# Where the selection work, the first-product halves and the gathers stand in a one-core PEER layer

## The chip, the cores and the metric

The kernel runs on one core of a Trainium2 chip. TensorE (PE) does the matrix products, VectorE (DVE) and ScalarE (ACT) the elementwise work, GpSimd (POOL) issues the gathers, SyncE (SP) issues the other DMAs; each engine takes its instructions in the order in which they stand. The metric is device microseconds of one execution; lower is better. Before the change the median of three runs is 3994.11 us (3992.14 to 4011.59).

## The reference

One layer is computed for 128 context tokens and 512 sample tokens with D = 2048. A mixer (input projection, a convolution branch, a two-way linear recurrence, output projection) is followed by PEER, a retrieval of experts out of 128 x 128:

```python
q = (xb @ w_query).reshape(TOKEN_BLOCK, PEER_HEADS, 2, D_KEY)
s = jnp.einsum('chpd,hpnd->chpn', q, sub_keys)
sv, si = lax.top_k(s, PEER_TOPK)                       # 16 best of 128 keys, both halves
cand = sv[:, :, 0, :, None] + sv[:, :, 1, None, :]     # 16 x 16 sums
top_s, top_pos = lax.top_k(cand, PEER_TOPK)            # 16 experts per head, 8 heads
ids = jnp.take_along_axis(cand_id, top_pos, axis=-1)
g = jax.nn.softmax(top_s, axis=-1)
act = gelu(einsum('chkd,cd->chk', jnp.take(peer_u, ids, axis=0), xb))
return einsum('chk,chkd->cd', g * act, jnp.take(peer_v, ids, axis=0))
```

Everything is in float32. A layer norm with residual closes each part.

## The kernel before

The tokens are in two groups. For group b (256 tokens, two tiles) experts are selected first; its first 192 tokens are **gathered tokens**: for each of their 128 experts per token a row of `peer_u` and a row of `peer_v` are fetched by indirect DMA (128 rows of 8 KB in one gather; 384 gathers, as the last 64 tokens share two halves of one tile). The other 448 sample tokens (64 of b, 384 of a) are done **densely**: all 16384 experts are multiplied, with a matrix of weights that is zero but for the selected ones.

After the mixer, PE goes through these stages:

1. The **first query** (`query(rpb, ...)`, group b, 32 halves of the query weights), with the output projection of group a between its halves, then the norm of group a.
2. The **second query** (`query(rpa, ...)`, group a, 32 halves; a half is 24 matmuls of 384 columns, lines 88 to 90).
3. The **first product**: 256 halves of `peer_uT` (24 matmuls of 448 columns each, `s_half`, lines 929 to 931). The generator `ahead_gen` issues one half for each `s_next()`. Two halves make one tile of 128 experts; ScalarE applies gelu (line 944) and SP writes the tile to DRAM (line 946). The first halves go to the PSUM tile `mm`, later ones to `sps`.
4. Part of these halves go beside the **one-hot matrices** (lines 977 to 1019): DVE and ACT build one-hot rows, PE multiplies them (line 1014), and the dense weights are written to `g_d` in 14 blocks. How many first-product halves stand between is worked out in line 995 from how many were already issued (`s_first`).
5. The **second product**, 256 halves of `peer_v` (lines 88 to 90 with the tile `vps`), which reads the gelu tiles (`ge`) and the weights (`gt`) back.

Every half of every weight is loaded by SP (line 82, 512 KB), split into a high part by ACT (line 76, `whi`) and a low part by DVE (line 77, `wlo`); PE needs both. There are two buffers of `whi` and `wlo` each, a third one for every third half.

**Selection** is DVE work: `tops` finds the 16 best of 128 keys, `choose` the 16 experts of a head, turns positions into numbers by comparing against 0..15 (`oh`), and writes `ids` and `gts`. It is cut into pieces, generators in a list `chores`; `chore(us)` adds a credit and issues pieces until their nominal costs (the numbers after `yield`) have used it up. The constants `C_WO`, `C_NA`, `C_QA`, `C_S` (line 759) are the credit for one half in each stage. When group b is selected, the piece `b_end` sets `b_done`; from there `pace(rate)` lets out gathers: `R_Q` = 0.4 for each half of the query and of the first product, 0.8 beside the one-hot matrices, and what is left, spread evenly, over the second product (`r_v`, line 1076). A gather of `peer_u` is followed by a dot product on DVE (line 853), one of `peer_v` by a sum on DVE (line 864). Three buffers hold gathered rows, so the third gather issued makes the oldest one be used; a gather also waits until PE has passed the half two before it (`after`, `LAG`).

The framework's scheduler orders the issued instructions on each engine; the order quoted below is the built one.

Of the kernel before, what the change touches and what calls it, by code (L numbers as in the profile page):

```python
# [34 lines left out]
def layer_kernel(ctx: ExitStack, tc: tile.TileContext, i: dict, y_p: bass.AP, y_s: bass.AP, st_o: bass.AP):  # L35
# [34 lines left out]
    def split(raw):  # L70
        n = raw.shape[1:]
        nsplit[0] += 1
        p = wx[0] if wx and nsplit[0] % 3 == 0 else w_p
        hi = p.tile([128, *n], F32R, name="whi", tag="whi")
        lo = p.tile([128, *n], F32R, name="wlo", tag="wlo")
        S.copy(hi, raw)  # L76
        V.tensor_tensor(lo, raw, hi.bitcast(F32), op=ALU.subtract)  # L77
        return hi, lo

    def load_w(src):  # L80
        raw = w_p.tile([128, *src.shape[1:]], F32, name="wraw", tag="wraw", bufs=3)
        Q.dma_start(raw, src)
        return raw
# [29 lines left out]
    def tp_bank():  # L113
        return ps_tp.tile([128, 512], F32, name="tp", tag="tp")

    def mm_bank():
        return ps_mm.tile([128, 512], F32, name="mm", tag="mm")
# [453 lines left out]
    def chore(us):  # L571
        credit[0] += us
        while chores and credit[0] > 0:
            try:
                credit[0] -= next(chores[0])
            except StopIteration:
                chores.pop(0)
        if not chores:
            credit[0] = min(credit[0], 0.0)
# [31 lines left out]
    def top16(rp, vals, idx, src, n):  # L611
        V.max(vals[:, 0:8], src)
        V.max_index(idx[:, 0:8], vals[:, 0:8], src)
        s2 = rp.tile([128, 128], F32, name="s2", tag="s2", bufs=1)
        V.match_replace(s2[:, 0:n], vals[:, 0:8], src, -3.0e38)
        V.max(vals[:, 8:16], s2[:, 0:n])
        V.max_index(idx[:, 8:16], vals[:, 8:16], s2[:, 0:n])

    def tops(rp, tv, ti, s, p, nt):
        for n in range(nt):  # L620
            top16(rp, tv[:, n, p, :], ti[:, n, p, :], s[:, n * 128:(n + 1) * 128], 128)
            yield 1.7

    def choose(rp, h, tv, ti, ts):
        nt = len(ts)

        def rt(shape, name, dt=F32, bufs=2):
            return rp.tile([128, *shape], dt, name=name, tag=name, bufs=bufs)

        cand = rt([nt, 112], "cand", bufs=1)  # L630
        for c0, a0, na, nb in ((0, 0, 4, 16), (64, 4, 12, 4)):
            V.tensor_tensor(
                cand[:, :, c0:c0 + na * nb].rearrange("p t (a b) -> p t a b", a=na),
                tv[:, :, 0, a0:a0 + na].unsqueeze(3).to_broadcast([128, nt, na, nb]),
                tv[:, :, 1, 0:nb].unsqueeze(2).to_broadcast([128, nt, na, nb]), op=ALU.add)
        yield 0.6
        tsv, tsp = rt([nt, 16], "tsv"), rt([nt, 16], "tsp", U32)
        for n in range(nt):
            top16(rp, tsv[:, n, :], tsp[:, n, :], cand[:, n, :], 112)
            yield 1.6  # L640
        nmx = rt([nt], "nmx")
        V.tensor_scalar(nmx, tsv[:, :, 0], -1.0, None, op0=ALU.mult)
        e, z = rt([nt, 16], "e"), rt([nt], "z")
        for n in range(nt):
            S.activation(e[:, n, :], tsv[:, n, :], AF.Exp, bias=nmx[:, n:n + 1], accum_out=z[:, n:n + 1])
        pu = rt([4, nt, 16], "pu", U32, bufs=1)
        pf = rt([4, nt, 16], "pf", bufs=1)
        V.tensor_scalar(pu[:, 0], tsp, 4, None, op0=ALU.logical_shift_right)
        V.tensor_scalar(pu[:, 1], tsp, 15, None, op0=ALU.bitwise_and)
        V.tensor_scalar(pu[:, 2], tsp, 2, None, op0=ALU.logical_shift_right)  # L650
        V.tensor_scalar(pu[:, 3], tsp, 3, None, op0=ALU.bitwise_and)
        S.copy(pf, pu)
        tif = rt([nt, 2, 16], "tif", bufs=1)
        S.copy(tif, ti)
        yield 0.9
        msk = rt([nt, 16], "msk")
        V.tensor_scalar(msk, pf[:, 0], 4.0, None, op0=ALU.is_ge)
        V.tensor_scalar(pf[:, 2], pf[:, 2], -12.0, None, op0=ALU.add)
        V.tensor_tensor(pf[:, 2:4], pf[:, 2:4], pf[:, 0:2], op=ALU.subtract)
        V.tensor_tensor(pf[:, 2:4], pf[:, 2:4], msk.unsqueeze(1).to_broadcast([128, 2, nt, 16]), op=ALU.mult)  # L660
        V.tensor_tensor(pf[:, 0:2], pf[:, 0:2], pf[:, 2:4], op=ALU.add)
        V.reciprocal(z, z)
        hk = slice(16 * h, 16 * h + 16)
        V.tensor_tensor(gts[:, ts[0]:ts[-1] + 1, hk], e, z.unsqueeze(2).to_broadcast([128, nt, 16]), op=ALU.mult)
        yield 1.5
        rs = []
        for p in range(2):
            oh = rt([nt, 16, 16], "oh", bufs=1)
            full = [128, nt, 16, 16]
            V.tensor_tensor(oh, pf[:, p].unsqueeze(3).to_broadcast(full),  # L670
                            iota[:, 0:16].unsqueeze(1).unsqueeze(1).to_broadcast(full), op=ALU.is_equal)
            yield 0.3 * nt
            V.tensor_tensor(oh, oh, tif[:, :, p, :].unsqueeze(2).to_broadcast(full), op=ALU.mult)
            yield 0.3 * nt
            r = rt([nt, 16], "r") if ts[0] == 0 else ij[:, 1:4, p, hk]
            V.tensor_reduce(r, oh, axis=AX.X, op=ALU.add)
            yield 0.3 * nt
            rs.append(r)
        if ts[0] == 0:
            for p in range(2):  # L680
                S.copy(ij[:, 0, p, hk], rs[p][:, 1, :])
            V.scalar_tensor_tensor(rs[0], rs[0], 128.0, rs[1], op0=ALU.mult, op1=ALU.add)
            V.tensor_copy(ids[:, :, hk], rs[0])
            yield 0.4

    def query(rp, uh, ul, ts, step, deep):
        nt = len(ts)
        N = nt * 128
        o = OFF if ts[0] else 0
        late = []  # L690
        for h in range(8):
            kT = rp.tile([128, 2, 128], F32, name="kT", tag="kT", bufs=2)
            Q.dma_start(kT, i["keysT"][:, 2 * h:2 * h + 2, :])
            tv = rp.tile([128, nt, 2, 16], F32, name="tv", tag="tv", bufs=deep)
            ti = rp.tile([128, nt, 2, 16], U32, name="ti", tag="ti", bufs=deep)
            for p in range(2):
                m = 2 * h + p
                bank = mm_bank()

                def scores(bank=bank, h=h, p=p, kT=kT, tv=tv, ti=ti):  # L700
                    qT = rp.tile([128, N], F32, name="qT", tag="qT", bufs=2)
                    S.copy(qT, bank[:, 0:N])
                    tp = tp_bank()
                    for n in range(nt):
                        T.matmul(tp[:, n * 128:(n + 1) * 128], qT[:, n * 128:(n + 1) * 128], kT[:, p, :], start=True, stop=True)
                    s = rp.tile([128, N], F32, name="s", tag="s", bufs=2 * deep - 1)
                    S.copy(s, tp[:, 0:N])
                    chores.append(tops(rp, tv, ti, s, p, nt))
                    if p:
                        chores.append(choose(rp, h, tv, ti, ts))  # L710

                for half in range(2):
                    raw = load_w(i["w_query"][m, :, half * 8:half * 8 + 8, :])
                    wh, wl = split(raw)
                    for kk in range(8):
                        k = half * 8 + kk
                        mk = mm3(bank[:, 0:N], wh[:, kk, :], wl[:, kk, :], uh[:, k, o:o + N], ul[:, k, o:o + N], k == 0, k == KT - 1)
                    marks.append(mk)
                    while late:
                        late.pop(0)()  # L720
                    step(2 * m + half)
                late.append(scores)
        while late:
            late.pop(0)()
# [31 lines left out]
                chores.insert(0, norm_a(*u2_a))  # L756
        chore(C_WO if not u2_a else C_NA)

    C_WO, C_NA, C_QA, C_S = 3.6, 2.8, 2.6, 2.8
    query(rpb, u2hi_b, u2lo_b, TB, step_b, 4)  # L760
    while len(chores) and chores[0].__name__ == "norm_a":
        chore(1.0)
# [9 lines left out]
    b_done = [False]  # L772
# [130 lines left out]
    R_Q, R_A = 0.4, 0.8  # L903
# [5 lines left out]
    def pace(n):  # L909
        if not b_done[0]:  # L910
            return
        due[0] += n
        while due[0] >= 1.0:
            due[0] -= 1.0
            left[0] -= 1
            next(gg, None)
# [18 lines left out]
    rate = [R_Q]  # L935
# [17 lines left out]
    def s_next():  # L953
        next(ag, None)
        nahead[0] += 1

    def step_a(n):
        pace(R_Q)
        chore(C_QA)

    query(rpa, u2hi_a, u2lo_a, TA, step_a, 4)
    while chores:
        s_next()
        chore(C_S)
# [239 lines left out]
```

## Time and profile before

| | |
|---|---|
| median of 3 runs | 3994.11 us (3992.14 to 4011.59) |
| profiled execution | 3995.82 us |
| its span | 3994.0 us |
| mean granted TensorE clock | 0.974 |
| PE busy | 3775.8 us, 95% |
| DVE busy | 3104.1 us, 78% |
| ACT busy | 1577.9 us, 40% |
| mean DMA rate | 264 GB/s |

The profile is of one execution; times in its rows are microseconds from the start of the span. PE busy is not PE at its peak: a matmul of 448 columns counts 369 ns, while back to back one starts about every 201.6 ns (249 in 50 us, or 1135 in 230 us). So lost time on PE is taken here as the length of a stretch less its matmuls at their back-to-back spacing, which also takes in stretches at the lower clock.

### The profile page before, as it was taken

How to read it: one execution, taken by the hardware profiler on the slowest of the kernel's cores; microseconds unless marked ns; L12 is line 12 of the kernel's file. 1: busy time of each engine (PE TensorE's matmuls, PEld its weight loads, DVE VectorE, ACT ScalarE, POOL GpSimd, SP SyncE). 2: the span in 40 equal slices, each digit the busy share in tenths (PEclk: the TensorE clock that was granted, in tenths of full speed). 3: DMA queues.
4: the chain of work that ended last, by engine and by line, in shares of the span. 5: the costliest groups of instructions: out<-in, count | busy, mean ns of one | idle time of the engine just before them, and what ended most of it. 6: DMA issues, size and time to landing. Idle time of an engine off the chain costs nothing.

```text
span 3994.0 us, 53950 instructions
## 1 busy us (share of the span) xinstructions
PE 3775.8 (95%) x20405; PEld 3355.1 (84%) x20405; DVE 3104.1 (78%) x4545; ACT 1577.9 (40%) x2697; POOL 742.3 (19%) x522
## 2 busy tenths in 40 slices
PE   7899899799999999999999999989999999999996
PEld 2688778678889999889998898979898988889886
DVE  5599965667899944688887787868888888888877
ACT  2111354533453322567675666632222222222221
POOL 0000111410000100112121222222332223332300
PEclk8899999899999999999999999999999999999998
DMA  9565444586533666788998788899999999999982
GB/s 365 204 203 182 152 142 161 185 256 227 167 127 111 213 214 216 256 319 302 321 316 301 275 289 306 314 345 357 337 352 330 355 339 333 347 332 358 330 239 89
DMA packets 408885, 1054.89 MB, mean 264 GB/s; under 512 B 27904, under 2 KB 253136, under 8 KB 355424
## 3 DMA queue, kind: packets, MB, share of 16 engines
q1 hardware_dynamic: 353328, 648.76, 48.5%
q0 software_dynamic: 55296, 402.68, 27.2%
q8 instruction: 160, 2.62, 0.3%
q14 instruction: 101, 0.83, 0.1%
HBM read 979.37 MB, written 71.38 MB: 263 GB/s over the span
## 4 chain that ended last, share of the span: by engine, by line
PE 53%; DMA 20%; DVE 15%; issue 7%; ACT 2%; POOL 1%; SPq 0%; DVEq 0%; POOLq 0%; ACTq 0%
PE sps L931 5%; PE sps L929 5%; PE sps L930 5%; PE vps L90 5%; PE vps L88 5%; PE vps L89 5%; DVE wlo L77 4%; DMA wa<-in_w_ada 4%; DMA ge<-ge_d 3%; DMA gt<-g_d 2%; DMA rows<-in_peer_v,ids 2%; DMA wraw<-in_peer_uT 2%; PE mm L931 2%; PE mm L930 2%; PE mm L929 2%
## 5 line engine op out<-in xcount | busy, mean ns | idle before, releaser
L76 ACT CAST whi<-wraw 128x1024 fp32r<-128x1024 f32 x704 | 736.8, 1049 | 1718.4 <-DMA wraw<-in_peer_v 380.9
L77 DVE TENSOR_TENSOR wlo<-wraw,whi 128x1024 fp32r<-128x1024 f32 x704 | 862.1, 1228 | 190.7 <-ACT whi L76 188.9
L853 DVE SCALAR_TENSOR_TENSOR rows<-rows,urow 128x2048 f32<-128x2048 f32 x192 | 439.1, 2287 | 187.2 <-DMA rows<-in_peer_u,ids 166.5
L929 PE MATMUL sps<-u2hi_a,whi 128*128 128x448 f32 x1488 | 548.9, 369 | 14.4 <-ACT whi L76 12.5
L864 DVE SCALAR_TENSOR_TENSOR gacc<-rows,coefs,gacc 128x2048 f32<-128x2048 f32 x190 | 445.9, 2347 | 146.7 <-DMA rows<-in_peer_v,ids 118.2
L931 PE MATMUL sps<-u2hi_a,wlo 128*128 128x448 f32 x1488 | 549.4, 369 | 7.9 <-DVE wlo L77 7.8
L930 PE MATMUL sps<-u2lo_a,whi 128*128 128x448 f32 x1488 | 547.6, 368 | 0.0
L88 PE MATMUL vps<-ehd,whi 128*128 128x448 f32 x1088 | 401.2, 370 | 15.6 <-ACT ehd L1055 10.6
L90 PE MATMUL vps<-ehd,wlo 128*128 128x448 f32 x1088 | 401.8, 369 | 6.8 <-DVE wlo L77 6.8
L89 PE MATMUL vps<-ehd,whi 128*128 128x448 f32 x1088 | 401.0, 369 | 0.0
L820 POOL DMA_INDIRECT rows<-in_peer_u,ids x128 | 184.2, 1439 | 1055.4 <-PE gps L1014 248.6
L90 PE MATMUL vps<-ehl,wlo 128*128 128x448 f32 x960 | 354.2, 369 | 20.8 <-DVE wlo L77 20.8
L88 PE MATMUL vps<-ehl,whi 128*128 128x448 f32 x960 | 352.2, 367 | 2.7 <-ACT whi L76 1.6
L89 PE MATMUL vps<-ehl,whi 128*128 128x448 f32 x960 | 351.9, 367 | 0.0
L929 PEld LDWEIGHTS sps<-u2hi_a,whi 128*128 128x128 f32 x1488 | 282.3, 190 | 38.0 <-ACT whi L76 13.7
L931 PEld LDWEIGHTS sps<-u2hi_a,wlo 128*128 128x128 f32 x1488 | 281.8, 189 | 37.4 <-DVE wlo L77 13.7
L930 PEld LDWEIGHTS sps<-u2lo_a,whi 128*128 128x128 f32 x1488 | 282.1, 190 | 22.2
L820 POOL DMA_INDIRECT rows<-in_peer_v,ids x128 | 197.3, 1541 | 533.9 <-PE gps L1014 162.9
L1010 ACT ACTIVATE A<-ab,gsp,nij 128x128 fp32r<-128x128 f32 x672 | 284.2, 487 | 1.6 <-DVE nij L991 1.5
L88 PEld LDWEIGHTS vps<-ehd,whi 128*128 128x128 f32 x1088 | 205.5, 189 | 35.4 <-ACT ehd L1055 11.0
L90 PEld LDWEIGHTS vps<-ehd,wlo 128*128 128x128 f32 x1088 | 205.4, 189 | 28.9 <-DVE wlo L77 10.9
L332 DVE SCALAR_TENSOR_TENSOR ybuf<-z,par,ybuf 128x655 f32<-128x655 f32 x240 | 220.6, 921 | 6.4
(301 smaller groups left out, 7514.8 us busy)
## 6 DMA issues: line engine op xcount, KB each, us to landing
wraw<-in_peer_uT SPq DMA_DIRECT2D x256, 512.0 KB
wraw<-in_peer_v SPq DMA_DIRECT2D x256, 512.0 KB
wa<-in_w_ada SPq DMA_DIRECT2D x192, 512.0 KB
wraw<-in_w_in SPq DMA_DIRECT2D x64, 512.0 KB
wraw<-in_w_out SPq DMA_DIRECT2D x64, 512.0 KB
wraw<-in_w_query SPq DMA_DIRECT2D x64, 512.0 KB
ge_d<-ge SPq DMA_DIRECT2D x128, 224.0 KB
g_d<-gst SPq DMA_DIRECT2D x14, 2048.0 KB
```

The source lines that it names most:

```text
L76: S.copy(hi, raw)
L77: V.tensor_tensor(lo, raw, hi.bitcast(F32), op=ALU.subtract)
L88: T.matmul(out, ah, bh, start=first, stop=False)
L89: T.matmul(out, ah, bl, start=False, stop=False)
L90: return T.matmul(out, al, bh, start=False, stop=last)
L820: d = G.indirect_dma_start(out=r, out_offset=None, in_=src, in_offset=bass.IndirectOffsetOnAxis(ap=idx, axis=0))
L853: V.scalar_tensor_tensor(r, r, 1.0, u, op0=ALU.mult, op1=ALU.mult, accum_out=dots[:, p:p + 1])
L864: V.scalar_tensor_tensor(acc, r, coef[:, p:p + 1], acc, op0=ALU.mult, op1=ALU.add)
L929: T.matmul(sps, wh[:, kk, :], u2hi_a[:, k, :], start=(k == 0), stop=False)
L930: T.matmul(sps, wh[:, kk, :], u2lo_a[:, k, :], start=False, stop=False)
L931: mk = T.matmul(sps, wl[:, kk, :], u2hi_a[:, k, :], start=False, stop=(k == KT - 1))
L1010: S.activation(A[:, x], ab, AF.Relu, scale=nij[:, 1 + x, n:n + 1], bias=gsp[:, x, n:n + 1])
```

## The change

The nominal costs of selection pieces change a little (a piece of `tops` 1.7 to 1.6, and so on), so a credit issues slightly more. The credit in the first query beside the output projection goes from 3.6 to 5.6. In the second query `step_a` has two cases: until group b is selected it issues a first-product half (`s_next`) and a credit of 8.0 for each query half; after that it lets out gathers and a credit of 3.3 (2.6 before). In the loop behind the query the credit is 4.2 (2.8) and the gather rate 0.45 (0.4).

```diff
@@ tops, choose (nominal costs of the pieces)
-            yield 1.7
+            yield 1.6
...
-            yield 1.6
+            yield 1.5
...
-        yield 0.9
+        yield 0.8
...
-        yield 1.5
+        yield 1.3
...
-            yield 0.3 * nt
+            yield 0.13 + 0.27 * nt
...
@@ -756,7 +756,7 @@
-    C_WO, C_NA, C_QA, C_S = 3.6, 2.8, 2.6, 2.8
+    C_WO, C_NA, C_QB, C_QA, C_S = 5.6, 2.8, 8.0, 3.3, 4.2
     query(rpb, u2hi_b, u2lo_b, TB, step_b, 4)
...
@@ -955,10 +955,15 @@
     def step_a(n):
-        pace(R_Q)
-        chore(C_QA)
+        if b_done[0]:
+            pace(R_Q)
+            chore(C_QA)
+        else:
+            s_next()
+            chore(C_QB)
 
     query(rpa, u2hi_a, u2lo_a, TA, step_a, 4)
+    rate[0] = 0.45
     while chores:
         s_next()
         chore(C_S)
```

In the built order of before, PE in the second query goes from one query half to the next, with the scores of the half-head (line 705) between:

```order
L88 MATMUL mm<-u2hi_a,whi 128x384
L89 MATMUL mm<-u2lo_a,whi 128x384
L90 MATMUL mm<-u2hi_a,wlo 128x384
L705 MATMUL tp<-kT,qT 128x128 x3
L88 MATMUL mm<-u2hi_a,whi 128x384
L89 MATMUL mm<-u2lo_a,whi 128x384
L90 MATMUL mm<-u2hi_a,wlo 128x384
```

In the changed kernel, at the same place on PE (lines 929 to 931 are the first product):

```order
L88 MATMUL mm<-u2hi_a,whi 128x384
L89 MATMUL mm<-u2lo_a,whi 128x384
L90 MATMUL mm<-u2hi_a,wlo 128x384
L705 MATMUL tp<-kT,qT 128x128 x3
L929 MATMUL mm<-u2hi_a,whi 128x448
L930 MATMUL mm<-u2lo_a,whi 128x448
L931 MATMUL mm<-u2hi_a,wlo 128x448
```

Ten first-product halves now stand between the first query halves, one each. In all, 36 halves of the first product come ahead of the one-hot matrices, where 70 did, and 220 beside them, where 186 did.

On DVE the first dot product of a gather (line 853) stands, before the change, behind the second query, among the first-product halves:

```order
L642 TENSOR_SCALAR nmx<-tsv 128x3
L612 MAX tv<-s 128x8
L853 SCALAR_TENSOR_TENSOR rows,dotss<-rows,urow 128x2048
L77 TENSOR_TENSOR wlo<-wraw,whi 128x1024
L616 MAX tsv<-s_13325 128x8
```

In the changed kernel the first one on DVE stands inside the second query, among the pieces of `tops`:

```order
L617 MAX_INDEX ti<-tv,s_11407 128x8
L613 MAX_INDEX ti<-tv,s 128x8
L853 SCALAR_TENSOR_TENSOR rows,dotss<-rows,urow 128x2048
L77 TENSOR_TENSOR wlo<-wraw,whi 128x1024
L615 MATCH_REPLACE s_11443<-tv,s 128x128
```

Counted in splits (line 77) from the first of the second query, the first dot product moves from behind the 38th to behind the 24th, and the last selection piece from behind the 53rd to behind the 61st. Gathers used on DVE ahead of the one-hot stage, beside it and in the second product: 26, 149 and 209 before, 20, 176 and 188 now. The selection instructions on DVE ahead of the first split of the second query are 211 in both.

On SP, in the same query, the loads before stand in fours behind each other:

```order
L82 DMA wraw<-in_w_query 128x1024 x3
L693 DMA kT<-in_keysT 128x256
L82 DMA wraw<-in_w_query 128x1024 x4
L693 DMA kT<-in_keysT 128x256
L82 DMA wraw<-in_w_query 128x1024
```

In the changed kernel SP has the loads of both weights in turn, and writes of gelu tiles (line 946) among them:

```order
L82 DMA wraw<-in_peer_uT 128x1024
L82 DMA wraw<-in_w_query 128x1024
L82 DMA wraw<-in_peer_uT 128x1024
L946 DMA ge_d_9949<-ge 128x448
L82 DMA wraw<-in_w_query 128x1024
L82 DMA wraw<-in_peer_uT 128x1024
```

A write waits for its gelu, and the loads behind it wait with it. ACT holds 18 table loads in the selection stretch, where it held 8.

## Rows read from the trace of the kernel before

**Rows 1.** The page: busy time by engine, and GB/s in 40 slices.
```profile
PE 3775.8 (95%) x20405; PEld 3355.1 (84%) x20405; DVE 3104.1 (78%) x4545; ACT 1577.9 (40%) x2697; POOL 742.3 (19%) x522
...
GB/s 365 204 203 182 152 142 161 185 256 227 167 127 111 213 214 216 256 319 302 321 316 301 275 289 306 314 345 357 337 352 330 355 339 333 347 332 358 330 239 89
```

**Rows 2.** Busy time by stretch: us, engines (instructions), granted clock, DMA share, GB/s.
```profile
core 0: us, PE busy (x) PEld busy (x) DVE busy (x) ACT busy (x) POOL busy (x), PEclk, DMA share, GB/s
1132.00:1286.00 154.00, 148.12 (x862) 146.25 (x863) 152.21 (x651) 61.01 (x139) 0.00 (x0) 0.98 0.37 120
1150.00:1200.00 50.00, 50.00 (x300) 50.00 (x299) 50.00 (x233) 18.53 (x44) 0.00 (x0) 1.00 0.38 125
1286.00:1400.00 114.00, 113.16 (x558) 103.61 (x557) 108.98 (x359) 44.79 (x75) 10.04 (x8) 1.00 0.60 201
1400.00:1630.00 230.00, 230.00 (x1135) 212.78 (x1135) 95.93 (x79) 59.61 (x71) 23.08 (x20) 1.00 0.64 221
1450.00:1500.00 50.00, 50.00 (x249) 46.34 (x248) 21.01 (x19) 13.61 (x17) 6.51 (x5) 1.00 0.65 225
1632.00:2640.00 1008.00, 980.00 (x4924) 898.86 (x4924) 791.87 (x878) 654.53 (x1407) 221.45 (x150) 0.99 0.87 305
2652.00:3780.00 1128.00, 1094.47 (x5292) 995.88 (x5291) 955.50 (x980) 297.33 (x359) 331.08 (x202) 0.99 0.95 342
```

**Rows 3.** Groups on DVE, 1132 to 1400: busy, mean ns, idle before.
```profile
L77 DVE TENSOR_TENSOR wlo<-wraw,whi 128x1024 fp32r<-128x1024 f32 x55 | 66.5, 1213 | 0.4 <-ACT whi L76 0.4
...
L853 DVE SCALAR_TENSOR_TENSOR rows<-rows,urow 128x2048 f32<-128x2048 f32 x8 | 18.3, 2282 | 3.1 <-DMA rows<-in_peer_u,ids 3.1
```

**Rows 4.** Waits of PE, 1132 to 1400: us in total, times, longest.
```profile
PE tp L705 <- ACT qT L702: 6.5, 4, 2.7
```

**Rows 5.** POOL in order of time, 1300 to 1306: the first gather.
```profile
1304.66 1.17 POOL L820 DMA_INDIRECT rows<-in_peer_u,ids  x1 [202.38 <-DVE wlo L77]
```

**Rows 6.** Groups on ACT, 1132 to 1400: table loads.
```profile
L944 ACT ACT_TABLE_LOAD x4 | 5.1, 1283 | 0.1
L645 ACT ACT_TABLE_LOAD x3 | 3.8, 1283 | 0.1
```

**Rows 7.** Waits of PE, one-hot stage, 1632 to 2640.
```profile
PE sps L929 <- ACT whi L76: 12.5, 4, 6.3
PE sps L931 <- DVE wlo L77: 7.8, 10, 1.6
```

**Rows 8.** Waits of PE, second product, 2640 to 3780.
```profile
PE vps L90 <- DVE wlo L77: 26.9, 29, 3.0
```

**Rows 9.** Groups on DVE, second product, 2652 to 3780.
```profile
L864 DVE SCALAR_TENSOR_TENSOR gacc<-rows,coefs,gacc 128x2048 f32<-128x2048 f32 x104 | 244.0, 2346 | 33.5 <-DMA rows<-in_peer_v,id 23.6 <-DMA rows<-in_peer_v,ids 9.6
L853 DVE SCALAR_TENSOR_TENSOR rows<-rows,urow 128x2048 f32<-128x2048 f32 x95 | 217.1, 2285 | 29.8 <-DMA rows<-in_peer_u,id 16.9 <-DMA rows<-in_peer_u,ids 9.2 <-DMA urow<-u_d 3.7
...
L1053 DVE TENSOR_TENSOR ge<-ge,gt 128x448 f32<-128x448 f32 x121 | 71.9, 620 | 100.4 <-DMA ge<-ge_d 52.8 <-DMA gt<-g_d 45.8 <-issue 1.6
```

**Rows 10.** The page's DMA queues: packets, MB, share of 16 engines.
```profile
q0 software_dynamic: 55296, 402.68, 27.2%
```

**Rows 11.** Waits of DVE, first product alone, 1400 to 1630.
```profile
DVE rows L853 <- DMA rows<-in_peer_u,ids: 71.0, 14, 7.6
```

More of the change, by code (lines that the diff above doesn't have):

```diff
@@ L671, in choose @@
                             iota[:, 0:16].unsqueeze(1).unsqueeze(1).to_broadcast(full), op=ALU.is_equal)
-            yield 0.3 * nt
+            yield 0.13 + 0.27 * nt
             V.tensor_tensor(oh, oh, tif[:, :, p, :].unsqueeze(2).to_broadcast(full), op=ALU.mult)
-            yield 0.3 * nt
+            yield 0.13 + 0.27 * nt
             r = rt([nt, 16], "r") if ts[0] == 0 else ij[:, 1:4, p, hk]
             V.tensor_reduce(r, oh, axis=AX.X, op=ALU.add)
-            yield 0.3 * nt
+            yield 0.13 + 0.27 * nt
             rs.append(r)
```

## The prediction

> **What bounds the kernel now.** I read the page first, then the table by stretch, then the waits and groups of the stretches that the change touches. The page shows PE busy for 95% of the span [rows 1], and no matmul is added or removed. So the change can only win back time that PE loses, or lose more, and the question is how much is lost in each stage and what loses it. I take lost time as the stretch less its matmuls at their closest spacing. That spacing is 50 us / 249 = 201 ns for 448 columns (the stretch 1400 to 1630, the same stage, gives 230 / 1135 = 202.6, and I use 201.6 in between) and 50 / 300 = 167 ns in the second query, scores included [rows 2].
>
> - Second query with selection, 1132 to 1286: 862 matmuls at 167 ns are 144 us of 154, so 10 us are lost. DVE is busy 152.2 of them and PE never waits long [rows 2]. DVE is the bound: a half needs its split, and the split stands behind selection pieces. The named wait of PE, for the copy ahead of the scores, is only 6.5 us to 1400 [rows 4].
> - First product with the rest of the selection, 1286 to 1400: 558 at 201.6 are 112.5 of 114 us, 1.5 lost, DVE 109.0 busy [rows 2].
> - First product alone, 1400 to 1630: 1.2 us lost. DVE is busy 96 of 230, DMA share 0.64 [rows 2].
> - Beside the one-hot matrices, 1632 to 2640: PE idles 1008 - 980 = 28 us, and a granted clock of 0.99 takes some 10 more: 38 us lost, DMA share 0.87 [rows 2]. The waits are for both halves of a split, 12.5 and 7.8 us [rows 7].
> - Second product, 2652 to 3780: 5292 at 201.6 are 1067 of 1128, 61 lost, at a DMA share of 0.95 and 342 GB/s [rows 2]. PE's wait here is for DVE's split, 29 times, 26.9 us [rows 8]. DVE is busy 955.5 us and waits 33.5, 29.8 and 100.4 us for gathered rows and for the tiles read back [rows 2, 9]: 1119 of 1128 us. Its queue is in order, so a late row also holds the split behind it.
>
> **The change part by part.** *Credit of the first query.* 211 selection instructions stand on DVE ahead of the second query in both orders: what a credit of 5.6 could issue isn't there yet. I cost it at nothing, and the new nominal costs of the pieces too, since what they do is in the counts below. If the few pieces that do move cost a stall, it is one split late, about 3 us (the longest wait for one in the second product was 3.0 [rows 8]); a gain is as large at most.
>
> *First-product halves inside the query.* Selection work on DVE from 1132 to 1400 is the busy time, 152.2 + 109.0 = 261, less 55 splits (66.5) and 8 dot products (18.3 and some 0.7 for reading them out) [rows 2, 3], so 176 us. The order before puts it beside 53 halves. DVE: 53 x 1.21 + 176 + 8 x 2.4 = 259 us. PE: 32 query halves with scores at 4.25 (51 matmuls at 167 ns for two) and 21 of the first product at 4.84 (24 at 201.6), 238 us. The excess of DVE is 21 us, and 11.5 are seen as lost; the other 9 or so are the halves that were split ahead. The new order puts the same selection beside 61 halves, 29 of them of the first product, and 17 dot products. DVE: 61 x 1.21 + 176 + 17 x 2.4 = 291. PE: 136 + 140 = 276. Excess 15, less the same 9: some 5 us lost. Gain 7 us. The bounds are 11.5 (no loss left) and 0 (excess unchanged, since the gathers move into the stretch as fast as room is made).
>
> *Rest of the first product.* The halves that ran alone go: 36 stand ahead of the one-hot stage instead of 70. That stretch lost 1.2 us, so nothing is won there. The one-hot work is spread over 220 halves instead of 186; gathers there stay at 0.80 for a half (176 / 220, 149 / 186). Two answers: the loss goes with the halves (38 x 34 / 186 = 7 us more), or with the 14 blocks, which are as many as before, while DVE has less to do for a half. Its 792 us for 186 halves are 4.26 us each; the one-hot part is 792 less 226 of splits and 149 x 2.4 of gathers, about 208, which falls from 1.12 to 0.95 us for a half. I take 0, from +7 (a loss) to -7.
>
> *Gathers earlier.* On DVE 188 of them stand in the second product where 209 did: 21 fewer. Each is 402.68 / 384 = 1.05 MB [rows 10], 22 MB together, out of 342 GB/s x 1128 us = 386 MB, so the DMA share falls by 5.7%, to about 0.90. On DVE 21 x 2.35 = 49 us go, and with them their share of the waits, 21 / 199 x 63 = 7 us [rows 9]. What PE wins lies between two bounds. If the loss goes with the number of gathers it is 61 x 0.10 = 6. If DVE and DMA set the pace of this stage, all 56 us come back, as far as PE allows (61 lost). On a straight line between the stretch alone (0.5% lost at a share of 0.64) and this one (5.4% at 0.95), a share of 0.90 costs 4.6%, and 9 us are won. Both the DVE load and the DMA load fall, and a loss that starts near saturation falls faster than a line, so I take 15. Since the rest is spread evenly, the end of the kernel stays where it was.
>
> The sum: -7 + 0 - 15 = -22 us against the profiled execution, 3995.8, so 3974. That execution lies 1.7 us above the median of the runs, so the forecast is 3972.
>
> **A page against a row.** The second product moves 342 GB/s on average, with slices to 358 [rows 1, 2]. The Trainium skill, "DMA: Bandwidth & Descriptors" (Specifications), gives about 358 GB/s as the limit of HBM for one core. By that figure the stage's 386 MB would take 1078 us and 364 MB 1017, and PE at 1067 would be the only bound left: the whole 61 us would come back. By the row it is not shown that the rate is a limit, for PE waits for DVE and not for loads; so this is a rival and not the sum.
>
> Ten table loads more stand on ACT in the selection stretch, where the row shows 1283 ns each [rows 6]: 13 us of ACT, which is busy 61 of 154 us there [rows 2] and has room. What stands behind such a load is the cast of a half and the copy ahead of the scores. The Trainium skill, "ScalarE: Activation LUTs" (What ACT_TABLE_LOAD costs), adds a drain and states 2.66 us for a switch; that would be 27 us of ACT. It speaks against the change; by it too ACT would be busy for less than the stretch, and the trace shows the load's 1283 ns alone.
>
> **The rivals.**
> 1. *The second product is set by DVE and DMA.* For it: DVE busy or waiting for 1119 of 1128 us, slices at 358 GB/s. Against: waits stretch when DVE has time. Then 56 instead of 15: 3995.8 - 7 - 56 = 3933, or 3931 for the median.
> 2. *What is won in the query is given back beside the one-hot matrices*, because 34 halves move from a stretch that loses nothing to one that loses. For it: 0.2 us for a half there (38 / 186). Against: fewer instructions of DVE and ACT for each half. -7 + 7 - 6 = -6: 3988 for the median.
> 3. *Slower: the gathers wait where DVE has no time.* 17 dot products now stand inside the stretch in which splits are late, and each waits for its row with the split behind it. For it: in the first product alone DVE waited 14 times, 71.0 us, 5.1 each [rows 11]. Against: those waits had a free DVE before them, and of the 8 that stood in the tight stretch one waited, 3.1 us [rows 3]. At 3.1 for each of 17 it would be 53 us on PE: +46 instead of -7, with -15 later, 4027, or 4025 for the median. It makes the kernel slower by over 20 us from 2.5 us a wait (17 x 2.5 = 42, which outweighs the 22 won).
> 4. *The table loads stand on the path.* Each delays a cast that PE needs: 13 us more, 3985. It would show as PE waiting for ACT. By the page it would be 27, and 3999.
>
> **How the numbers follow.** Forecast 0.60, with a range of its own of 3958 to 3986; rival 1 0.14, rival 2 0.15, rival 3 0.08, rival 4 0.03. The range takes the forecast and rival 2 and reaches down two thirds of the way to rival 1: 3944 to 3996. About 0.5% (20 us) is what a measurement can tell from no change, so faster means under 3974. Half of the forecast's weight (0.32) and rival 1 (0.14) lie there, with a little of rival 2: 0.48. Within 0.5% are the other half, most of rival 2 and rival 4: 0.44. Slower is rival 3: 0.08.
>
> **What would show it.** In the changed profile: the first gather on POOL 50 us or more earlier than 1304.7 [rows 5]; the stretch in which DVE is fully busy longer, with PE losing about 5 us in it; the one-hot stage starting some 160 us earlier (34 halves at 4.84) and taking as much longer, with about as much idle time of PE; the second product at a DMA share near 0.90 with PE waiting for splits clearly less than 26.9 us. I am wrong if DVE waits for rows in the second query for more than a few us in total, if PE's idle time beside the one-hot matrices grows by more than 10 us, or if the second product keeps its 61 us at the lower share.

## The result and the profile after

The changed kernel takes 3968.91 us (median of 8 runs, 3956.81 to 3978.33), the kernel before in the same comparison 4011.72 us (8 runs, 3992.14 to 4014.95). The ratio is 0.990, with a 95% interval from 0.9878 to 0.9921: faster by 1.0%. The forecast was 3972 us.

The profiled execution took 3971.66 us, with a span of 3969.9 us and a mean granted clock of 0.975. That is 24 us less than the profiled execution of before (3995.82), which was one of the quicker runs of that kernel. What follows divides these 24 us; the medians lie 43 us apart, and what the other 19 come from is not shown.

The page of the changed kernel, busy time by engine and GB/s in 40 slices, answers to [rows 1], and its software queue to [rows 10]:

```profile
PE 3770.2 (95%) x20405; PEld 3349.8 (84%) x20405; DVE 3111.5 (78%) x4545; ACT 1593.6 (40%) x2707; POOL 726.0 (18%) x522
...
GB/s 360 207 204 183 148 142 160 175 262 237 158 136 177 203 240 303 307 310 321 312 311 307 315 305 306 317 335 308 335 313 322 329 342 310 341 321 340 310 229 89
...
q0 software_dynamic: 55296, 402.68, 27.4%
```

The same work, 5.6 us less of PE busy, and over 300 GB/s is reached in slice 16 instead of 18.

The table by stretch of the changed kernel (us, engines with their instructions, granted clock, DMA share, GB/s), for [rows 2]. The stretches are: second query with selection, first product with selection, a little first product, beside the one-hot matrices, second product.

```profile
1136.00:1337.00 201.00, 197.96 (x1107) 192.29 (x1107) 196.55 (x760) 88.96 (x173) 12.06 (x9) 0.98 0.50 167
1337.00:1400.00 63.00, 62.69 (x311) 57.35 (x310) 62.69 (x205) 26.51 (x42) 8.16 (x6) 1.00 0.64 216
1400.00:1467.00 67.00, 66.22 (x325) 60.43 (x323) 47.98 (x91) 21.27 (x31) 7.62 (x7) 1.00 0.72 242
1468.00:2612.00 1144.00, 1134.90 (x5735) 1043.04 (x5733) 892.63 (x951) 696.47 (x1454) 271.66 (x175) 1.00 0.89 311
2628.00:3753.00 1125.00, 1092.48 (x5273) 993.62 (x5272) 911.70 (x948) 297.44 (x359) 277.03 (x183) 0.99 0.91 325
```

Beside the one-hot matrices PE idles 9 us in 1144, where it idled 28 in 1008, and the clock is full. In the second product 5273 matmuls at 201.6 ns are 1063 of 1125 us: 62 us are lost, as before (61), though the DMA share fell from 0.95 to 0.91.

The waits of PE in the changed kernel (us in total, times, longest), for [rows 4, 7, 8]: in the selection, beside the one-hot matrices, and in the second product:

```profile
PE tp L705 <- ACT qT L702: 3.0, 1, 3.0
...
PE sps L931 <- DVE wlo L77: 5.6, 9, 1.2
PE gps L1019 <- DVE A L1018: 2.0, 1, 2.0
...
PE vps L90 <- DVE wlo L77: 23.4, 21, 2.4
```

The 12.5 us of waits for `whi` beside the one-hot matrices [rows 7] have no line any more.

For the whole table I add up, from start to start of successive matmuls, what each gap has over the closest spacing of its kind (448 columns 201.6 ns, 384 columns 167.5, 256 columns 117). This loss includes what is lost at the lower of TensorE's two clock levels (1.2 instead of 2.4 GHz, a granted clock of 0.50). The first one-hot matrix is counted from the transposes just ahead of it:

| us lost by PE | before | after | difference | forecast |
|---|---|---|---|---|
| ahead of the second query | 135.6 | 139.2 | +4 | 0 |
| second query to the first one-hot matrix | 21.4 | 17.5 | -4 | -7 |
| beside the one-hot matrices | 53.6 | 27.1 | -26 | 0 |
| between the products | 10.8 | 13.2 | +2 | 0 |
| second product | 67.3 | 67.2 | 0 | -15 |

The sum was nearly right, and two of its terms were not: the gain lies in the stage for which I had forecast none.

### The profile page after: what moved, and what is told of

The parts are those of the page before. It is cut to its first block, busy times and chain, and to the rows that moved or that the text cites. A ratio compares the mean times of both kernels' runs of the same rounds, so it can differ in the third digit from the quotient of the medians.

```text
span 3969.9 us, 53949 instructions
## 1 busy us (share of the span) xinstructions
PE 3770.2 (95%) x20405; PEld 3349.8 (84%) x20405; DVE 3111.5 (78%) x4545; ACT 1593.6 (40%) x2707; POOL 726.0 (18%) x522
## 4 chain that ended last, share of the span: by engine, by line
PE 54%; DMA 20%; DVE 15%; issue 8%; ACT 2%; POOL 2%; SPq 0%; DVEq 0%; POOLq 0%; ACTq 0%
PE sps L931 6%; PE sps L930 6%; PE sps L929 6%; PE vps L90 6%; PE vps L88 6%; PE vps L89 6%; DVE wlo L77 4%; DMA wa<-in_w_ada 4%; DMA rows<-in_peer_v,ids 3%; DMA ge<-ge_d 2%; DMA gt<-g_d 2%; DMA wraw<-in_peer_uT 2%; PE adab L156 2%; PE mm L258 2%; PE mm L256 2%
## 5 line engine op out<-in xcount | busy, mean ns | idle before, releaser
L931 PE MATMUL sps<-u2hi_a,wlo 128*128 128x448 f32 x1760 | 645.2, 367 | 5.8 <-DVE wlo L77 5.6
L929 PE MATMUL sps<-u2hi_a,whi 128*128 128x448 f32 x1760 | 644.5, 366 | 0.2 <-ACT ge L944 0.2
L930 PE MATMUL sps<-u2lo_a,whi 128*128 128x448 f32 x1760 | 644.1, 366 | 0.0
L931 PEld LDWEIGHTS sps<-u2hi_a,wlo 128*128 128x128 f32 x1760 | 330.3, 188 | 38.8 <-DVE wlo L77 10.0
L929 PEld LDWEIGHTS sps<-u2hi_a,whi 128*128 128x128 f32 x1760 | 330.4, 188 | 27.4 <-ACT ge L944 0.6
L930 PEld LDWEIGHTS sps<-u2lo_a,whi 128*128 128x128 f32 x1760 | 330.3, 188 | 26.9
```

The costliest lines, as they stand in the source:

```text
L929: T.matmul(sps, wh[:, kk, :], u2hi_a[:, k, :], start=(k == 0), stop=False)
L930: T.matmul(sps, wh[:, kk, :], u2lo_a[:, k, :], start=False, stop=False)
L931: mk = T.matmul(sps, wl[:, kk, :], u2hi_a[:, k, :], start=False, stop=(k == KT - 1))
```

## The experiments

Lost time is counted as in the table. The kernels are edits of the changed kernel unless something else is said. Ratios are against the kernel before, on the same chip.

**Which part of the one-hot stage pays.** Three theories at first: the one-hot work is spread over more first-product halves; one engine has too much to do for each half; or the writes of the weight blocks (`g_d`) stand in the way.

*dense*: 34 first-product halves are again issued alone, ahead of the one-hot stage.

```diff
     while chores:
         s_next()
         chore(C_S)
+    while nahead[0] < 69:
+        s_next()
     rate[0] = R_A
     s_first = nahead[0]
```

> The changed kernel, but 34 further first-product halves run alone before the one-hot stage, so that its one-hot work stands beside about 186 halves, as before the change. Theory D (the one-hot work that DVE and ACT have for each half sets the loss there): the loss in that stage comes back from 27 us to about 50, the kernel is some 25 us slower than the changed one, about 0.995 of the kernel before. Rival G (the earlier gathers made the gain): the loss there stays near 27 us, and the time stays near that of the changed kernel, 0.99.

Measured: 3995.0 us, ratio 0.998 (0.9961 to 0.9998). The loss beside the one-hot matrices is 38.9 us instead of 27.1, half way between what theory D (50) and rival G (27) wanted, and that of the second product 80.8 instead of 67.2. With the halves put back most of the gain is gone, although the selection and the query are as in the changed kernel.

*gdve2* and *gdve0*: of four one-hot rows DVE builds two, or none, instead of one; ACT builds the others. The edit of gdve2 (gdve0 has 0):

```diff
-    G_MOD, G_DVE = 4, 1
+    G_MOD, G_DVE = 4, 2
```

> The changed kernel with two of four one-hot rows built by DVE instead of one: 224 more pairs' worth of DVE time (about 58 us, 0.26 us for a half, back to the load of before) and some 150 us less on ACT. If DVE's load for a half sets the loss in the one-hot stage (theory D, DVE part), the loss rises from 27 to about 50 us, ratio 0.995. If ACT's load sets it (theory D, ACT part), it falls below 27 us, ratio 0.985 to 0.99.

> The changed kernel with no one-hot row built by DVE: 58 us less on DVE, 150 us more on ACT in the one-hot stage. If DVE's load sets the loss there, it falls below 20 us, ratio 0.985 to 0.99. If ACT's load sets it, it rises to 50 us or more, ratio 0.995 or above.

Measured: 3956.66 us, ratio 0.9891 (0.9862 to 0.992), and 3971.8 us, 0.9921 (0.9897 to 0.9946). The stage loses 25.8 and 28.4 us: moving a quarter of the rows from one engine to the other changes next to nothing, so neither engine alone sets this loss.

*both*: in each group of four, one row is built twice on DVE and another twice on ACT (224 more instructions on DVE and 336 on ACT; measured, 58 us more busy time on DVE and 106 on ACT in the stage).

```diff
-                        for x in range(2):
+                        for x in (0, 1, 0, 1) if tt_ == 1 else (0, 1):
                             S.activation(A[:, x], ab, AF.Relu, scale=nij[:, 1 + x, n:n + 1], bias=gsp[:, x, n:n + 1])
...
-                        for x in range(2):
+                        for x in (0, 1, 0, 1):
                             V.tensor_scalar(A[:, x], iota, ijgT[:, 0, n:n + 1], gsp[:, x, n:n + 1], op0=ALU.is_equal, op1=ALU.mult)
```

> The changed kernel with one of four one-hot rows built twice on DVE and another one twice on ACT, in the same place: some 58 us more on DVE and 154 us more on ACT in the one-hot stage, so that both engines have more to do for a half than before the change. Theory L (the load of the two engines together sets the loss there): the loss of the stage rises from 27 us to 50 or more. Theory W (the weight blocks written to DRAM) and theory P (how one-hot products fall between the halves): it stays below 33.

Measured: 3984.56 us (before 4017.15, one run each); the stage loses 45.8, between the 50 that theory L wanted and the 33 of the others. Load costs something, 19 us in this one run, but the longest wait of PE there is 2.7 us.

*dblw*: each weight block is written twice.

```diff
+            for _ in range(2):
                 Q.dma_start(g_d[:, :, blk], st.rearrange("p (g x) t -> p g x t", x=4))
```

> The changed kernel with each of the 14 blocks of dense weights written twice to the same place (29 MB more in small pieces). Theory W: the loss of the one-hot stage rises from 27 us to 50 or more. Theories L and P: it stays below 35.

Measured: 4049.77 us (before 4017.15, one run each); the stage loses 126.9 us, and for 96 us of the stage PE runs at the 1.2 GHz level. The waits of PE in that stage (1468 to 2713):

```profile
PE sps L929 <- ACT whi L76: 44.7, 8, 10.6
PE sps L929 <- ACT ge L944: 29.6, 6, 6.1
```

The first is the form of wait that stood at the head of [rows 7] and that the change removed. So the block writes can make PE wait in just this way. The question left was why 14 writes cost so much before and so little after.

**Is it the number of halves?** 69 halves stand ahead of the one-hot stage before the change, 35 in the changed kernel (36 on PE). My theory S was that the loss falls with the number that is left for the stage. Three kernels set it otherwise; the first two are edits of the kernel before.

*inter* (59 halves ahead): the halves between the query's halves alone.

```diff
     def step_a(n):
-        pace(R_Q)
-        chore(C_QA)
+        if b_done[0]:
+            pace(R_Q)
+            chore(C_QA)
+        else:
+            s_next()
+            chore(8.0)
```

> The kernel before, with one part of the change: a first-product half stands behind each query half (credit 8.0) until group b is selected; all other credits and nominal costs as before. 59 halves then stand ahead of the one-hot stage (before 69, changed kernel 35). Theory S (the gain comes with the number of halves that are left for the one-hot stage): 10 of the 34 halves, so about 10/34 of the 24 us, 7 us, ratio 0.996 to 1.000, the one-hot stage still losing 42 to 54 us. Rival Q (the placing inside the query is what pays, by DVE's tight stretch): the ratio is 0.990 to 0.993, and the loss of the selection stretch falls by 10 us or more.

Measured: 3978.11 us, ratio 0.9931 (0.9896 to 0.9966). The stage loses 42.1 us, the selection stretch 16.6.

*cred* (39 halves ahead): the credits alone.

```diff
-    C_WO, C_NA, C_QA, C_S = 3.6, 2.8, 2.6, 2.8
+    C_WO, C_NA, C_QA, C_S = 5.6, 2.8, 3.3, 4.2
```

> The kernel before, with the other part alone: the credits 5.6, 3.3 and 4.2, no first-product half in the query, old nominal costs. 39 halves then stand ahead of the one-hot stage (before 69, changed kernel 35). Theory S: 30 of the 34 halves, so most of the gain, ratio 0.990 to 0.994, the one-hot stage losing 26 to 34 us instead of 54. Rival Q: ratio 0.998 to 1.002. A third way: the heavier credit makes the selection stretch lose 10 us or more beyond its 21 and eats the gain, which would be the reason for placing halves inside the query.

Measured: 3974.12 us, ratio 0.9911 (0.988 to 0.9943). The stage loses 47.8 us, the selection stretch 19.8. By the times, the credits alone bring most of the gain and the halves inside the query alone a good part of it; but the loss of the stage does not follow the number of halves. Of the 17 us by which cred's profiled execution is shorter than that of before, only 6 lie in this stage and 10 in the second product (57.6 us lost).

*wo36* (37 halves ahead): the changed kernel with the old credit of the first query.

```diff
-    C_WO, C_NA, C_QB, C_QA, C_S = 5.6, 2.8, 8.0, 3.3, 4.2
+    C_WO, C_NA, C_QB, C_QA, C_S = 3.6, 2.8, 8.0, 3.3, 4.2
```

> The changed kernel with the credit of the first query back at 3.6. 37 halves then stand ahead of the one-hot stage (35 in the changed kernel). If that credit is worth nothing, as forecast, the ratio is 0.988 to 0.993, as for the changed kernel. If it paid for some of the gain, 0.994 or more.

Measured: 4025.44 us (4023.45 to 4038.94, 4 runs), ratio 1.0048 (1.0016 to 1.0081): slower than the kernel before. Nearly all of it is in the one-hot stage, which loses 83.7 us and runs for 51 us at the lower clock; selection (15.2) and second product (71.4) are near the changed kernel's 17.5 and 67.2. The longest waits of PE in that stage (1472 to 2664):

```profile
PE sps L929 <- ACT ge L944: 22.8, 7, 5.7
PE sps L929 <- ACT whi L76: 9.4, 3, 5.2
```

They are of the forms of dblw, and the changed kernel has 0.2 us of them. Theory S has fallen: two halves more or less ahead of the stage cannot cost 56 us by their number.

**What two halves shift.** They move the place of the block write among the loads in SP's queue. That can be counted in the order of the instructions alone: the loads of `peer_uT` ahead of a block's write on SP, less the halves ahead of that block's last one-hot matmul on PE. In wo36 it is five loads at all 14 writes, in the changed kernel six at 13 of them and five at the last, in the kernel before five at 12 and six at two. SP in order of time (start, us, line, transfer), around the first block write (line 1024), first in the changed kernel:

```profile
1547.68 0.33 SPq L82 DMA_DIRECT2D wraw<-in_peer_uT  x1
1548.74 0.60 SPq L1024 DMA_DIRECT2D g_d<-gst  x1
1554.52 8.16 SPq L82 DMA_DIRECT2D wraw<-in_peer_uT  x1
1562.74 0.42 SPq L946 DMA_DIRECT2D ge_d<-ge  x1
```

and in wo36:

```profile
1544.77 0.33 SPq L82 DMA_DIRECT2D wraw<-in_peer_uT  x1
1550.74 0.60 SPq L1024 DMA_DIRECT2D g_d<-gst  x1
1551.40 9.09 SPq L946 DMA_DIRECT2D ge_d<-ge  x1
1560.58 2.16 SPq L82 DMA_DIRECT2D wraw<-in_peer_uT  x3
```

In both, the first transfer issued behind the 2 MB write holds SP for 8 or 9 us instead of 0.3 to 0.4. In wo36 that is a gelu write, and the loads stand behind it. The next cast on ACT in each (start, us, in brackets the idle time and what ended it), the changed kernel:

```profile
1569.70 1.05 ACT L76 CAST whi<-wraw 128x1024 fp32r<-128x1024 f32 x1 [6.71 <-DMA wraw<-in_peer_uT]
1570.65 0.54 ACT L944 ACTIVATE ge<-sps 128x448 f32<-128x448 f32 x1
```

wo36:

```profile
1572.07 1.04 ACT L76 CAST whi<-wraw 128x1024 fp32r<-128x1024 f32 x1 [14.93 <-DMA wraw<-in_peer_uT]
1573.02 0.54 ACT L944 ACTIVATE ge<-sps 128x448 f32<-128x448 f32 x1
```

The cast begins 21 us behind the write in both, when its load has landed. But in wo36 ACT had nothing left to cast for 14.9 us, in the changed kernel for 6.7, and the gelu that frees PE's buffer stands behind that cast. PE in wo36 at that time:

```profile
1567.58 0.37 PE L931 MATMUL sps<-u2hi_a,wlo 128*128 128x448 f32 x1
1573.61 0.74 PE L929 MATMUL sps<-u2hi_a,whi 128*128 128x448 f32 x1 [5.67 <-ACT ge L944]
```

PE stops for 5.7 us, and the next matmul takes 0.74 us instead of 0.37. The clock has fallen to its lower level: in the stretch 1574 to 1578 the granted clock is 0.50, and the matmuls in it start 0.37 us apart instead of 0.20.

```profile
1574.00:1578.00 4.00, 4.00 (x12) 3.30 (x12) 4.00 (x6) 3.97 (x11) 0.00 (x0) 0.50 0.53 188
...
1574.97 0.57 PE L929 MATMUL sps<-u2hi_a,whi 128*128 128x448 f32 x1
1575.34 0.57 PE L930 MATMUL sps<-u2lo_a,whi 128*128 128x448 f32 x1
```

The kernel before has the same picture. SP around the block write that its longest wait follows (line 1019 there):

```profile
2240.66 0.53 SPq L1019 DMA_DIRECT2D g_d<-gst  x1
2241.80 13.24 SPq L82 DMA_DIRECT2D wraw<-in_peer_uT  x2
```

and the cast that waits for it:

```profile
2263.76 1.04 ACT L76 CAST whi<-wraw 128x1024 fp32r<-128x1024 f32 x1 [16.04 <-DMA wraw<-in_peer_uT]
```

PE then waited the 6.3 us of [rows 7].

I call *reserve* the halves whose load SP has issued up to a block write, less the halves that PE has begun (with fractions). For the 14 writes of each kernel, with PE's loss from 8 to 45 us behind each:

| kernel | halves ahead | mean reserve (range) | loss behind the writes | writes with over 2 us | loss of the stage |
|---|---|---|---|---|---|
| before | 69 | 3.8 (3.1 to 5.0) | 39.5 | 6 | 53.6 |
| after | 35 | 4.7 (3.8 to 5.2) | 14.8 | 1 | 27.1 |
| wo36 | 37 | 3.6 (3.2 to 4.0) | 64.3 | 10 | 83.7 |
| cred | 39 | 4.1 (3.2 to 5.4) | 23.3 | 5 | 47.8 |
| inter | 59 | 4.0 (3.4 to 5.1) | 19.9 | 3 | 42.1 |
| dense | 69 | 3.9 (3.2 to 5.0) | 25.8 | 2 | 38.9 |

With gdve0, gdve2 and both (above) and gedeep and best (below) there are 154 such writes. At a reserve under 4 halves (52 writes) the mean loss is 3.5 us, and 28 lose over 2; from 4 halves on (102 writes) it is 1.1, and 8 do. The place in the order sorts them as well: with five loads ahead (62 writes) the mean loss is 3.3 us and 30 lose over 2, with six (92 writes) 1.0, and 6 do. The six writes of before that lose over 2 us, the ten of wo36 and the one of the changed kernel all have five. From before to after, 25 of the stage's 26 us lie behind the block writes. In cred and inter 24 and 22 us lie elsewhere, against 12 to 14 in these two, some of them at waits for one-hot rows; why is open. So is why a write with five loads ahead costs 4.6 us on average in wo36 and 3.2 in before, but 1.6 to 2.2 in cred, inter and dense. The table compares kernels that differ in other things too. That block writes can make PE lose this much is shown by dblw; that one constant changes their place and brings the loss back, by wo36 and its rows. A kernel in which only the block write changes its place in SP's queue was not run, so how much of the 26 us the place alone is worth is read from the table and not from such a kernel.

**What the second product loses.** Four kernels.

*nogath*: no gathers in the second product, and none of their dot products and sums, which are missing in the output.

```diff
         def gather(src, idx):
+            if skip[0]:
+                return None
...
         bufs_ = (ehd, ehl)
+        skip[0] = True
         for x in range(sizes[0]):
```

> The changed kernel without the gathers of the second product: the remaining rows are neither fetched nor used, so the result for the gathered tokens lacks them. If gathers set the loss of the second product, it falls from 67 us (to the stage's last matmul) to below 25. If the tiles read back set it (theory R), it stays above 40, as DVE still waits for them with the splits behind.

*noread*: the gelu tiles and weights are read back only for the first tiles and used again for all others, so the others are missing in the output.

```diff
-            if e < NE and e not in loads:
+            if e > 2:
+                loads[e] = loads[e % 3]
+            elif e not in loads:
```

> The changed kernel without the reading back of the gelu tiles and the dense weights but for the first few: the second product uses the first tiles again, so the dense tokens' result is not the reference's. Theory R: the loss of the second product falls from 67 us to below 30. If gathers set it: DVE's waits move to the gathered rows and the loss stays above 45.

Measured: 3925.15 and 3919.2 us (before 4017.15, one run each). The second product loses 16.7 and 18.1 us instead of 67.2. The stretch 2640 to 3740, nogath:

```profile
2640.00:3740.00 1100.00, 1100.00 (x5397) 1012.54 (x5396) 560.42 (x700) 305.59 (x355) 1.12 (x2) 1.00 0.51 165
```

noread:

```profile
2640.00:3740.00 1100.00, 1098.61 (x5388) 1010.72 (x5387) 932.54 (x956) 300.52 (x352) 279.82 (x185) 1.00 0.84 291
```

Noread has all 186 gathers and the same DVE load (932.5 us busy), and PE idles for 1.4 us. So neither the gathers nor DVE's load make the loss by themselves; the gathers and the reading back do together. Nor do long waits of DVE: in noread it still waits 160 us for gathered rows, and PE loses 18.

*gedeep*: six buffers for the tiles read back instead of three, loaded four ahead instead of one (a norm's weights are loaded later to make room).

```diff
-                loads[e] = gep.tile([128, ND], F32, name="ge", tag="ge")
+                loads[e] = dp.tile([128, ND], F32, name="ge2", tag="ge2", bufs=3) if e % 2 else gep.tile([128, ND], F32, name="ge", tag="ge")
...
-            load_ge(e + 1)
+            for a in (1, 2, 3, 4):
+                load_ge(e + a)
```

> The changed kernel with six buffers instead of three for the gelu tiles that the second product reads back, loaded four tiles ahead instead of one. Theory R (the second product kept its loss because DVE waits there for tiles read back, 118 us, with the splits queued behind): DVE's wait for them falls below 50 us, the loss of the second product from 62 to about 40 us, ratio about 0.985. Rival (the loss follows the gathers, or is in the matmuls' spacing): the waits move to the gathered rows and the loss stays near 60 us, ratio 0.99.

Measured: 3939.16 us (3936.41 to 3941.55, 4 runs), ratio 0.9838 (0.9815 to 0.9861): faster than both kernels. The second product loses 37.5 us. The same stretch, gedeep:

```profile
2640.00:3740.00 1100.00, 1087.43 (x5307) 997.01 (x5306) 917.41 (x947) 296.24 (x352) 280.55 (x184) 1.00 0.93 334
```

at a higher DMA share than the changed kernel's 0.91. The groups on DVE in the second product (busy, mean ns, idle before and its causes), the changed kernel, for [rows 9]:

```profile
L864 DVE SCALAR_TENSOR_TENSOR gacc<-rows,coefs,gacc 128x2048 f32<-128x2048 f32 x95 | 222.9, 2347 | 46.1 <-DMA rows<-in_peer_v,id 31.4 <-DMA rows<-in_peer_v,ids 14.7
L853 DVE SCALAR_TENSOR_TENSOR rows<-rows,urow 128x2048 f32<-128x2048 f32 x85 | 194.3, 2286 | 30.9 <-DMA rows<-in_peer_u,id 22.7 <-DMA rows<-in_peer_u,ids 8.0
...
L1058 DVE TENSOR_TENSOR ge<-ge,gt 128x448 f32<-128x448 f32 x119 | 70.8, 621 | 118.3 <-DMA ge<-ge_d 60.2 <-DMA gt<-g_d 54.3 <-issue 3.6
```

and in gedeep:

```profile
L864 DVE SCALAR_TENSOR_TENSOR gacc<-rows,coefs,gacc 128x2048 f32<-128x2048 f32 x97 | 227.8, 2348 | 69.6 <-DMA rows<-in_peer_v,id 44.5 <-DMA rows<-in_peer_v,ids 24.6 <-DVE vaccT L1126 0.5
L853 DVE SCALAR_TENSOR_TENSOR rows<-rows,urow 128x2048 f32<-128x2048 f32 x85 | 194.4, 2287 | 49.2 <-DMA rows<-in_peer_u,id 37.6 <-DMA rows<-in_peer_u,ids 11.4
...
L1059 DVE TENSOR_TENSOR ge<-ge,gt 128x448 f32<-128x448 f32 x114 | 66.3, 618 | 51.1 <-DMA gt<-g_d 51.0
```

DVE's 60 us of waits for `ge` are gone, and DVE waits longer for rows instead. PE's wait for splits in that stretch of gedeep:

```profile
PE vps L90 <- DVE wlo L77: 7.6, 6, 1.9
```

It was 23.4 us. DVE's idle time in these three groups only falls from 195 to 170 us, but it is taken at other places now, and less of it reaches PE; which property of a wait decides that was not tried.

*best*: gedeep and gdve2 together.

> The changed kernel with the six buffers for gelu tiles and four loads ahead (gedeep), and two in four one-hot rows built on DVE instead of one (gdve2). If the two gains are separate (second product 30 us, one-hot stage 1 to 2 us), the ratio is 0.980 to 0.985, the loss of the second product 30 to 45 us, and that of the one-hot stage 25 to 33. If the two loads stand in each other's way, 0.986 to 0.990.

Measured: 3941.34 us (3934.32 to 3959.32, 4 runs), ratio 0.9838 (0.9801 to 0.9875), no better than gedeep alone. Its profiled run, the longest of the four, loses 35.9 us beside the one-hot matrices and 47.6 in the second product. Gdve2 adds nothing that can be measured.

## Why the prediction was right and where it was wrong

- *Credit of the first query: nothing.* For the selection itself this holds: with either credit 15 to 20 us are lost there, and few pieces move (the last one stands behind the 63rd split in wo36, behind the 61st in the changed kernel). As a price it fails: wo36 undoes this one constant and is 1.4 to 1.5% slower than the changed kernel. I had only priced its own work and not that it shifts every later block write.
- *First-product halves inside the query: -7.* Measured -4 (21.4 to 17.5, up to the one-hot matrices and counted gap by gap, where the prediction saw 11.5 in its two stretches), between the bounds of 0 and -11.5. The view of DVE as the bound of that stretch was right: it is busy 196.55 of 201 us.
- *Rest of the first product and the one-hot stage: 0, from +7 to -7.* This step failed: -26. Already its start was low, 38 us lost where the table counts 53.6. I weighed the loss by the number of halves or by DVE's instructions for a half. The runs show a third thing, the 14 block writes and their place in SP's queue, behind which 25 of the 26 us are won; I read the waits of [rows 7] as DVE and ACT being late and did not follow the 6.3 us wait back to its load, for which ACT waits 16 us behind a block write. The stage did start 164 us earlier (1468 for 1632), as forecast. That chain could have been read before.
- *Gathers earlier: second product -15.* In the two profiles 0: the sign I had named as a failure came, the stage kept its 61 us at the lower share, and PE's wait for splits is 23.4 us where I wanted clearly less than 26.9. Over more kernels with this stage unedited it looks otherwise: with 198 to 206 gathers there 67.3, 68.9 and 80.8 us are lost (before, inter, dense; mean 72), with 186 to 191 from 48.5 to 71.4 (after, gdve0, gdve2, both, dblw, wo36, cred; mean 59). The 13 us between the means are near the forecast, but runs with the same gathers lie 20 us apart, so this is not settled.
- *Rival 1* (all 56 us come back) did not happen. It rested on the rate: the Trainium skill, "DMA: Bandwidth & Descriptors" (Specifications), gives about 358 GB/s as HBM's limit for a core. The trace does not bear it out as the bound here: the stage lost as much at 325 GB/s as at 342, and gedeep lost 30 us less at 334. Nor is DVE, busy or waiting, the bound: in gedeep that is still 1087 of 1100 us (917 busy, 170 waiting), as it was 1119 of 1128 before. Asking for each tile earlier was worth 30 us there. And 358 is not where the rate ends in this trace: the first slice of [rows 1] moves 365 GB/s.
- *Rival 2* (given back beside the one-hot matrices): the opposite came.
- *Rival 3* (gathers wait where DVE has no time): not seen. POOL issued the first gather 66 us earlier than in [rows 5]:

```profile
1238.56 1.83 POOL L820 DMA_INDIRECT rows<-in_peer_u,ids  x1 [133.28 <-DVE oh L670]
```

and DVE's waits for such rows in the changed kernel from 1136 to 1467, with the few gathers that stand there, are:

```profile
DVE rows L853 <- DMA rows<-in_peer_u,ids: 7.5, 3, 5.5
DVE gacc L862 <- DMA rows<-in_peer_v,ids: 3.6, 1, 3.6
DVE gacc L864 <- DMA rows<-in_peer_v,ids: 3.4, 1, 3.4
```

14.5 us with the rows of `peer_v`, where the rival wanted 53; only 2.0 of them lie ahead of 1400, where DVE has no time to spare.
- *Rival 4* (table loads): 17 loads now stand in that stretch, as the groups on ACT show, for [rows 6]:

```profile
L944 ACT ACT_TABLE_LOAD x9 | 11.5, 1283 | 0.2
L645 ACT ACT_TABLE_LOAD x8 | 10.3, 1283 | 0.1
```

and PE waited for ACT once, 3.0 us. They did not reach the path.

The total was met because a gain that I had not seen stood in for one that the profiled pair did not show. That the time agrees within 3 us is luck, twice over: the forecast took 22 us from a median of 3994, and in the comparison the kernel before has 4012, so the measured gain is 43 us by the medians, nearly twice the forecast.

## What to carry to other kernels

A constant that shifts work by a place or two can move a large write against the loads in the same queue; when the time jumps with a small edit, list for each such write how many loads are ahead of the consumer, before explaining it by the work that was moved. A wait for a cast or a split is followed back to the load behind it, and from there to what the queue issued just ahead. Where an engine works in order and waits for tiles that are asked for just in time, loading them further ahead can pay by itself: in gedeep it saved 30 of the second product's 67 us and brought the time from 0.990 to 0.984 of the kernel before, while the 20 gathers that the change took out of that stage saved nothing in the profiled pair.

## What was not expected of the hardware

- Behind a 2 MB write the next transfer held SP's queue for 3.1 to 14.1 us (the 14 writes of the changed kernel; 4.0 to 13.5 in wo36). Of the 315 other transfers in that stage of the changed kernel one held it over 2 us, and the median is 0.33. ACT could begin on the awaited 512 KB some 21 us behind the write, in the changed kernel as in wo36.
- A stop of PE of 5.7 us was followed by matmuls at the 1.2 GHz level (one in 0.37 us instead of 0.20). In the one-hot stage 27 us lay at that level before, none after, 51 in wo36 and 96 in dblw. Since nearly half of such time is lost, that is some 24 of the 84 us of wo36, an estimate from these two spacings.
- The loss of the second product rose steeply with the DMA share: 17 us at 0.51, 18 at 0.84, 67 at 0.91; but gedeep lost 37.5 at 0.93, so the share alone does not set it.
- The kernel before varied by 0.8% from run to run (3990.52 to 4021.35 on one chip, 7 runs), gedeep by 0.13% (3936.41 to 3941.55, 4 runs); best, which has gedeep's edit too, by 0.6% (3934.32 to 3959.32, 4 runs).
